# First weights ahead of x, six products ahead of the second tile's transposes, a 22nd weight buffer, and rows numbered by partition in a hybrid attention and expert layer

## The chip, the cores and the metric

The kernel runs on one core of one Trainium2 chip. The metric is the device time of one execution in microseconds (us). The kernel before took 678.57 us (median of 3 runs, 677.72 to 679.63). The engines are TensorE (PE; its weight loads are listed apart as PEld), VectorE (DVE), ScalarE (ACT), GpSimd (POOL) and SyncE (SP), which in this kernel only issues transfers.

## The reference

One layer: two attention branches side by side, merged by gates, and then a mixture of experts. T = 512 tokens, D = 1024, everything in float32.

```python
h = rmsnorm(x, attn_norm)
proj = h @ w_in                                  # one wide product, split into eight parts
c_q, c_kv, k_r, q_b, k_b, v_b, gate_a, gate_b = split(proj)
o_a = mla_attention(c_q, c_kv, k_r, ...)         # 8 heads, low-rank q and kv, causal
o_b = moba_attention(q_b, k_b, v_b, ...)         # 8 heads, causal, block-sparse
x = x + (sigmoid(gate_a) * (o_a @ w_o_mla) + sigmoid(gate_b) * (o_b @ w_o_moba)) @ w_out
x = x + hierarchical_moe(rmsnorm(x, ffn_norm))   # group top-1, then expert top-2 of 8 in the group
return rmsnorm(x, final_norm)

# an expert e, for the tokens routed to it (32 experts in 4 groups, 1024 -> 256 -> 1024)
y = (silu(xb @ w_g[e]) * (xb @ w_u[e])) @ w_d[e]
out[token] += weight * y
```

## The kernel before

Tokens are worked on in four tiles of 128. Float32 products outside the experts are made of three products each: every operand is split into a high part (`hi`) and a low part (`lo`), and hi times hi, hi times lo and lo times hi are added up in PSUM. The high part is cast on ACT, the low part is the rest, made on DVE.

**Start** (`normed_T`, L166 to L185). The tiles of x (x0 to x3, 512 KB each) and three pieces of the first weights (w0 and w1 of two rows of 128 by 352, 352 KB each, and w2 of four, 704 KB) go through SP's queue in the order x0 w0 x1 w1 x2 x3 w2. PE first makes twelve transposes of a constant, then transposes each tile of x (eight blocks of 128 by 128, in two groups of four: "A" and "B"; L206), ACT and DVE split each group (`evac_split`, L44 and L45), and `split` (L65 and L66) splits the weights. The products of the first projection (`proj`, L95 to L97) follow in `mla_compress`. On SP, ACT and DVE the order in this part is as written. PE's order is chosen by the scheduler.

**Middle.** From 14 to 434 us come the projections, both attentions, the gates, the output projection and, tile by tile, the routing (class `Route`), which writes the normed rows to a table in DRAM (`x2d`) and, at the end, the table of routing weights (`Wd`, L591). Small loads for it (`load_late`: the router weights `wr`, the gains `gpj` and `gcol`, the biases and the table of constants `rc`) go through SP early, and the scaling of `wr` on DVE follows them.

**Experts** (`experts`, 434 to 660 us). The 32 experts run as sixteen pairs, q = 0 to 15, with up to 64 tokens for each expert of a pair. A pair needs six weight matrices of 1 MB (gate, up and down for two experts), 96 loads in all, issued by SP into a ring of buffers (`new_w`): the loads of a pair go gate, gate, up, up, down, down, those of pairs 0 to 2 ahead of the loop, those of pair q + 2 at the start of pair q. A load also waits until the third load before it has landed (`load`). The ring has 21 buffers; those numbered 11, 12, 13, 14 and 19 take space of the pool `wp`, which held the split weights until then, and the sixth buffer of that pool is `yhl`, the split output of the experts. For each pair PE transposes the gathered rows (L765), makes the gate and the up products (`gate_up`, L788), transposes the activation (L800) and makes the down products (L815). Pairs in `VIA` send their output through DRAM. The others (0, 3, 6 and 10 to 15) add theirs to x2 with a one-hot matrix S: a combine is two products (L841 and L842) for one half of the columns of one tile, eight combines a pair. The combines of a pair are made during the next pair: `some(n)` makes the next n of those left over.

**End** (`last`). After the last down products the output is split on ACT and DVE (L822, L823), combined, and normed with `final_norm`, whose load goes behind the last weights on SP and which ACT scales first (L973). In this part the order on ACT and DVE is as written.

## Time and profile before

| what | value |
|---|---|
| runs: median, lowest, highest | 678.57, 677.72, 679.63 us |
| the profiled execution | 677.66 us |
| its span in the trace | 675.9 us (1.76 us lie outside it) |
| PE, DVE, ACT, POOL busy | 97%, 53%, 42%, 13% |
| data moved | 155.37 MB, mean 230 GB/s |
| DMA busy share, 7.76 to 434 us and 448 to 652 us | 0.48 and 1.01 |

The profile is taken from one execution; its times are microseconds from the first instruction. A row of a timeline gives the start, the time that the instructions took together (matmuls are pipelined, so that the ends overlap), the engine, the line of the kernel, the operation with its output and inputs, the count, and in brackets the idle time of the engine just before with what ended it. "SPq" and "ACTq" are the queues that issue transfers; the time in such a row is that of issuing. The landing of a transfer is counted from its issue.

### The profile page before, as it was taken

To read this page: it belongs to the slowest core of one execution; us is meant where nothing else is said; L and a number is where in the kernel's file an instruction comes from. 1 tells how busy PE (TensorE), PEld (TensorE's weight loads), DVE (VectorE), ACT (ScalarE), POOL (GpSimd) and SP (SyncE) were. 2 spreads that over 40 slices of the span, in tenths; PEclk is the share of its full clock that TensorE was granted. 3 is DMA by queue.
4 is the path that set the end of the run, shared out by engine and by line. 5 is a ranking of instruction groups with operands and counts; after the bars stand their busy time and mean duration, and the time that the engine had idled before them with its cause. 6 is when DMAs were issued, how large, how long until landed. Compare 5 with 4: busy or idle time off the path is not lost.

```text
span 675.9 us, 11016 instructions
## 1 busy us (share of the span) xinstructions
PE 656.0 (97%) x4150; PEld 502.9 (74%) x4150; DVE 360.5 (53%) x928; ACT 284.9 (42%) x657; POOL 88.2 (13%) x136
## 2 busy tenths in 40 slices
PE   8999999999999999999999999999999999989992
PEld 7998887777788888888888899855566566656551
DVE  4525957877947993434477323733223213556646
ACT  5747545654638683433324143323222222212234
POOL 1504000000000000000000001212112212334303
PEclk9999999999999999999999999999999999999997
DMA  8734451801073028231298957799999999999963
GB/s 264 139 87 73 84 172 63 280 1 63 10 199 104 1 64 249 63 93 63 98 339 300 387 201 262 275 355 417 404 404 419 418 407 409 407 409 408 415 260 128
DMA packets 76041, 155.37 MB, mean 230 GB/s; under 512 B 32270, under 2 KB 54886, under 8 KB 64144
## 3 DMA queue, kind: packets, MB, share of 16 engines
q1 hardware_dynamic: 67424, 141.59, 57.9%
q0 software_dynamic: 5232, 7.98, 3.5%
q10 hardware_dynamic: 3328, 5.05, 2.7%
q8 instruction: 34, 0.56, 0.3%
q14 instruction: 23, 0.19, 0.1%
HBM read 153.24 MB, written 11.60 MB: 244 GB/s over the span
## 4 chain that ended last, share of the span: by engine, by line
PE 86%; DMA 9%; DVE 2%; ACT 1%; POOL 1%; issue 1%; SPq 0%; ACTq 0%
PE yp L815 7%; PE U L788 7%; PE G L788 7%; PE pacc L97 5%; PE pacc L96 5%; PE pacc L95 5%; PE pacc L456 4%; PE pacc L454 4%; PE pacc L455 4%; DMA w<-in_w_exp_gate_dram 4%; DMA w<-in_w_exp_up_dram 4%; PE ptr L425 3%; PE S L407 3%; PE O L433 2%; PE pacc L498 2%; PE pacc L500 2%
## 5 line engine op out<-in xcount | busy, mean ns | idle before, releaser
L66 DVE SCALAR_TENSOR_TENSOR wlo<-wraw,ms,whi 128x256 fp32r<-128x256 f32 (+2 forms) x134 | 68.2, 551 | 30.8 <-ACT whi L65 30.6
L65 ACT ACTIVATE whi<-wraw,ms 128x256 fp32r<-128x256 f32 (+2 forms) x134 | 67.0, 560 | 41.7 <-PE pacc L455 19.8
L95 PE MATMUL pacc<-whi,hThi 128*128 128x352 f32 (+1 forms) x192 | 72.4, 377 | 0.0
L794 DVE SCALAR_TENSOR_TENSOR a<-U,wg,a 128x256 f32<-128x256 f32 x15 | 10.3, 686 | 115.4 <-PE U L788 89.1
L97 PE MATMUL pacc<-whi,hTlo 128*128 128x352 f32 (+1 forms) x192 | 70.1, 365 | 0.0
L96 PE MATMUL pacc<-wlo,hThi 128*128 128x352 f32 (+1 forms) x192 | 70.0, 365 | 0.0
L788 PE MATMUL U<-w,xT 128*64 128x256 f32 x512 | 61.0, 380 | 2.8 <-DMA w<-in_w_exp_up_dram 2.8
L815 PE MATMUL yp<-w,a 128*64 128x512 f32 x256 | 58.5, 598 | 0.5 <-ACT a L802 0.5
L788 PE MATMUL G<-w,xT 128*64 128x256 f32 x512 | 58.0, 379 | 0.0
L788 PEld LDWEIGHTS G<-w,xT 128*64 128x64 f32 x512 | 36.7, 137 | 24.9 <-issue 4.6
L788 PEld LDWEIGHTS U<-w,xT 128*64 128x64 f32 x512 | 37.4, 137 | 23.1 <-DMA w<-in_w_exp_up_dram 4.7
L454 PE MATMUL pacc<-hThi,whi 128*128 128x512 f32 x128 | 50.3, 393 | 0.0
L456 PE MATMUL pacc<-hThi,wlo 128*128 128x512 f32 x128 | 50.3, 393 | 0.0
L455 PE MATMUL pacc<-hTlo,whi 128*128 128x512 f32 x128 | 49.9, 390 | 0.0
L1169 POOL TENSOR_SCALAR sq<-sq 128x1 f32<-128x1 f32 x4 | 0.9, 218 | 343.5 <-ACT junk L1166 343.5
L420 ACT ACTIVATE E<-E,mx 128x128 f32<-128x128 f32 (+3 forms) x64 | 35.6, 557 | 20.4 <-DVE mx L417 19.6
L843 DVE TENSOR_TENSOR x<-x,cp 128x512 f32<-128x512 f32 x64 | 40.0, 682 | 2.0 <-PE cp L842 2.0
L95 PEld LDWEIGHTS pacc<-whi,hThi 128*128 128x128 f32 x192 | 36.1, 188 | 4.9 <-issue 1.4
L815 PEld LDWEIGHTS yp<-w,a 128*64 128x64 f32 x256 | 17.0, 136 | 30.2 <-issue 27.8
L96 PEld LDWEIGHTS pacc<-wlo,hThi 128*128 128x128 f32 x192 | 36.2, 189 | 4.2 <-issue 0.7
L97 PEld LDWEIGHTS pacc<-whi,hTlo 128*128 128x128 f32 x192 | 36.1, 188 | 3.9 <-issue 0.2
L802 ACT COPY a<-G 128x256 f32<-128x256 f32 x16 | 6.0, 373 | 75.2 <-PE G L800 59.0
(245 smaller groups left out, 1354.3 us busy)
## 6 DMA issues: line engine op xcount, KB each, us to landing
w<-in_w_exp_gate_dram SPq DMA_DIRECT2D x32, 1024.0 KB, 8.2
w<-in_w_exp_up_dram SPq DMA_DIRECT2D x32, 1024.0 KB, 8.1
w<-in_w_exp_down_dram SPq DMA_DIRECT2D x30, 1024.0 KB, 8.4
wraw<-in_w_in_dram SPq DMA_DIRECT2D x14, 1024.0 KB, 5.2
wraw<-in_w_out_dram SPq DMA_DIRECT2D x4, 1024.0 KB, 7.3
wraw<-in_w_in_dram SPq DMA_DIRECT2D x5, 704.0 KB, 4.8
xs<-in_x_dram SPq DMA_DIRECT2D x4, 512.0 KB, 6.6
wraw<-in_w_o_mla_dram SPq DMA_DIRECT2D x4, 512.0 KB, 3.5
```

Of the source, the lines that this page charges most:

```text
L65: nc.scalar.mul(hi[:, k], raw[:, k], g)
L66: nc.vector.scalar_tensor_tensor(lo[:, k], raw[:, k], g, hi[:, k].bitcast(F32), ALU.mult, ALU.subtract)
L95: nc.tensor.matmul(ps[t][:, :ncols], act_hi[kk // 4][:, kk % 4, ts], hi[:, k], start=kk == 0, stop=False)
L96: nc.tensor.matmul(ps[t][:, :ncols], act_hi[kk // 4][:, kk % 4, ts], lo[:, k], start=False, stop=False)
L97: nc.tensor.matmul(ps[t][:, :ncols], act_lo[kk // 4][:, kk % 4, ts], hi[:, k], start=False, stop=kk == ktot - 1)
L420: nc.scalar.activation(E, E, AF.Exp, bias=mx, scale=-1.0, accum_out=sm)
L454: nc.tensor.matmul(ps, hi[:, k, ds], self.hT[0][k // 4][:, k % 4], start=k == 0, stop=False)
L455: nc.tensor.matmul(ps, hi[:, k, ds], self.hT[1][k // 4][:, k % 4], start=False, stop=False)
L456: nc.tensor.matmul(ps, lo[:, k, ds], self.hT[0][k // 4][:, k % 4], start=False, stop=k == KD - 1)
L788: nc.tensor.matmul(GU[i][es, 0:256], xT[:, j, es], gu[e][i][:, j * 256:(j + 1) * 256], start=j == 0, stop=j == KD - 1)
L815: nc.tensor.matmul(yp[es], aT[:, j, es], wd[e][:, j * D + half * 512:j * D + half * 512 + 512], start=j == 0, stop=j == 1)
L843: nc.vector.tensor_tensor(self.x2[t][:, hs], self.x2[t][:, hs], cp, ALU.add)
```

## The change

The change has five edits.

- The start sends w0 ahead of x0, so that SP's order is w0 x0 x1 w1 x2 x3 w2. The split of w0 moves ahead of x0's on ACT and DVE. The six products of token tile 0 with w0 (`proj_part`, taken out of `proj`) are written ahead of the second tile's transposes, and a dependence (`earlier`) holds the first of these transposes until the sixth product has ended.
- The pool `wp` ends with the middle part, and its space becomes six buffers of a pool `wx`. Five of them are those of the ring as before. The sixth, `w3`, takes the second up matrix of pair 0, loaded behind the other seventeen loads of pairs 0 to 2, and becomes `yhl` after pair 0's products.
- In pairs whose predecessor left eight combines and is later than the last of `VIA` (pairs 11 to 15), four combines are made between the gate and the up products.
- The rows of the tables `Wd` and `x2d` are numbered by partition (row 4p + t for token p of tile t) instead of by tile (128t + p); the constants `token` and `tm` follow, and `tm` gets 64 more columns.
- Two pads change so that the addresses fit.

```diff
     def proj(self, w, groups, act_hi, act_lo, ncols, evac, gain):
-        ps = [self.acc.tile([P, 512], F32, name="pacc", tag="acc") for _ in range(NT)]
+        first, self.first_ps = self.first_ps, None
+        ps = first or self.new_sums()
...
+                if not (first and k0 == t == 0):
+                    self.proj_part(ps[t][:, :ncols], t, range(k0, k0 + nk), hi, lo, act_hi, act_lo, ktot)
...
+    def proj_part(self, ps, t, ks, hi, lo, act_hi, act_lo, ktot):
+        nc = self.nc
+        ts = slice(t * P, (t + 1) * P)
+        for k, kk in enumerate(ks):
+            nc.tensor.matmul(ps, act_hi[kk // 4][:, kk % 4, ts], hi[:, k], start=kk == 0, stop=False)
+            nc.tensor.matmul(ps, act_hi[kk // 4][:, kk % 4, ts], lo[:, k], start=False, stop=False)
+            mm = nc.tensor.matmul(ps, act_lo[kk // 4][:, kk % 4, ts], hi[:, k], start=False, stop=kk == ktot - 1)
+        return mm
...
-            for t in range(NT):
-                nc.sync.dma_start(xs[t // 2][:, t % 2], io["x"][0, t * P:(t + 1) * P, :])
-                if t != 2:
+            for t in ("w", 0, 1, "w", 2, 3, "w"):
+                if t == "w":
                     k, n = groups[len(raw)]
                     raw.append(self.load_raw(self.w_in_view(CC // 3 * 2, CC // 3)(k, n), (n, CC // 3)))
+                else:
+                    nc.sync.dma_start(xs[t // 2][:, t % 2], io["x"][0, t * P:(t + 1) * P, :])
...
+            self.first_w.append(self.split(raw[0], g[:, 0, 0:2]))
+            mm = None
             for t in range(NT):
                 x = xs[t // 2][:, t % 2]
-                self.transpose_split(x[:, 0:512], 4, self.hT, 0, t)
-                if t < 2:
-                    self.first_w.append(self.split(raw[t], g[:, 0, 2 * t:2 * t + 2]))
+                self.transpose_split(x[:, 0:512], 4, self.hT, 0, t, mm)
+                if t == 0:
+                    self.first_ps = self.new_sums()
+                    mm = self.proj_part(self.first_ps[0][:, 0:CC // 3], 0, range(2), *self.first_w[0], *self.hT, KD)
+                if t == 1:
+                    self.first_w.append(self.split(raw[1], g[:, 0, 2:4]))
                 self.started = self.transpose_split(x[:, 512:D], 4, self.hT, 4, t)
...
-            nc.scalar.dma_start(self.Wd.rearrange("(t p) c -> p t c", p=P), self.W)
+            nc.scalar.dma_start(self.Wd.rearrange("(p t) c -> p t c", p=P), self.W)
...
-        pool, tag = {11: (self.wp, "wraw"), 12: (self.wp, "wraw"), 13: (self.wp, "whi"), 14: (self.wp, "wlo"),
-                     19: (self.wp, "wlo")}.get(i, (self.big, "big"))
-        return pool.tile([P, 2048], F32, name="w", tag=tag)
+        at = {11: 0, 12: 1, 13: 2, 14: 4, 19: 5}.get(i)
+        if at is not None:
+            return self.wx.tile([P, 2048], F32, name="w", tag=f"w{at}")
+        return self.big.tile([P, 2048], F32, name="w", tag="big")
...
-            ws = [[self.load_rows(io[n][0, e]) for e in range(2)] for n in ("w_exp_gate", "w_exp_up")]
-            return list(zip(*ws))
+            g = [self.load_rows(io["w_exp_gate"][0, e]) for e in range(2)]
+            return [(g[0], self.load_rows(io["w_exp_up"][0, 0])), (g[1], self.wx.tile([P, 2048], F32, name="w", tag="w3"))]
...
-        self.yhl = self.wp.tile([P, 2048], F32R, name="yhl", tag="whi")
+        self.load_rows(self.io["w_exp_up"][0, 1], wgu[0][1][1])
...
+                    if j == KD - 1 and len(todo) == 8 and q - 1 not in VIA and q > VIA[-1]:
+                        some(4)
...
+                if q == 0:
+                    self.yhl = self.wx.tile([P, 2048], F32R, name="yhl", tag="w3")
...
-        nc.scalar.dma_start(L.x2d[self.ts, c0:c1], self.x2[:, c0:c1])
+        nc.scalar.dma_start(L.x2d.rearrange("(p t) c -> p t c", p=P)[:, self.t, c0:c1], self.x2[:, c0:c1])
...
-    rc[:, 33:33 + NT] = np.arange(P)[:, None] + P * np.arange(NT)[None, :] - 1024
+    rc[:, 33:33 + NT] = NT * np.arange(P)[:, None] + np.arange(NT)[None, :] - 1024
```

Line numbers of the changed kernel differ: L206 becomes L221, L95 to L97 become L106 to L108, L788 becomes L806, L841 and L842 become L859 and L860, L697 becomes L715.

PE's order at the start, before (`ptr<-ident` are transposes of the constant, `ptr<-ident,xs` those of x, `pacc` the products of the first projection):

```order
1 L160 MATMUL ptr<-ident 128x128 x12
2 L206 MATMUL ptr<-ident,xs 128x128 x12
3 L95 MATMUL pacc<-whi,hThi 128x352
4 L206 MATMUL ptr<-ident,xs 128x128 x4
5 L96 MATMUL pacc<-wlo,hThi 128x352
6 L97 MATMUL pacc<-whi,hTlo 128x352
7 L95 MATMUL pacc<-whi,hThi 128x352
8 L96 MATMUL pacc<-wlo,hThi 128x352
9 L97 MATMUL pacc<-whi,hTlo 128x352
10 L95 MATMUL pacc<-whi,hThi 128x352
11 L96 MATMUL pacc<-wlo,hThi 128x352
12 L206 MATMUL ptr<-ident,xs 128x128 x4
```

And in the changed kernel:

```order
1 L169 MATMUL ptr<-ident 128x128 x12
2 L221 MATMUL ptr<-ident,xs 128x128 x8
3 L106 MATMUL pacc<-whi,hThi 128x352
4 L107 MATMUL pacc<-wlo,hThi 128x352
5 L108 MATMUL pacc<-whi,hTlo 128x352
6 L106 MATMUL pacc<-whi,hThi 128x352
7 L107 MATMUL pacc<-wlo,hThi 128x352
8 L108 MATMUL pacc<-whi,hTlo 128x352
9 L221 MATMUL ptr<-ident,xs 128x128 x12
10 L106 MATMUL pacc<-whi,hThi 128x352
11 L107 MATMUL pacc<-wlo,hThi 128x352
12 L106 MATMUL pacc<-whi,hThi 128x352
```

Before, x0's and half of x1's transposes stood ahead of the first product. Now the six products stand between x0's eight transposes and the twelve of x1 and x2's first half.

SP's queue of expert loads around the last loads of pairs 0 to 2, before (`w_4369` is the second up matrix of pair 0; `w_4397` is the last down matrix of pair 2, and `w_4508` the first gate matrix of pair 3):

```order
86 L697 DMA w_4367<-in_w_exp_up_dram 128x8x256 [waits PE_49]
87 L697 DMA w_4369<-in_w_exp_up_dram 128x8x256 [waits Pool_49]
...
106 L697 DMA w_4395<-in_w_exp_down_dram 128x2048 [waits DMAHW6_49,PE_49]
107 L697 DMA w_4397<-in_w_exp_down_dram 128x2048 [waits DMAHW0_49,DMAHW4_49,PE_49,Pool_49]
108 L697 DMA w_4508<-in_w_exp_gate_dram 128x2048 [waits DMAHW2_49,PE_49,Pool_49]
109 L697 DMA w_4510<-in_w_exp_gate_dram 128x2048 [waits DMAHW6_49,PE_49]
110 L697 DMA w_4512<-in_w_exp_up_dram 128x2048 [waits DMAHW5_49,DMAHW0_49]
```

And in the changed kernel (`w_4379` is that second up matrix, `w_4518` the first gate matrix of pair 3):

```order
85 L715 DMA w_4377<-in_w_exp_up_dram 128x8x256 [waits PE_49]
86 L715 DMA w_4380<-in_w_exp_down_dram 128x2048 [waits Pool_49]
...
105 L715 DMA w_4406<-in_w_exp_down_dram 128x2048 [waits DMAHW6_49,DMAHW2_49,PE_49]
106 L715 DMA w_4379<-in_w_exp_up_dram 128x8x256 [waits DMAHW7_49,DMAHW3_49,PE_49]
107 L715 DMA w_4518<-in_w_exp_gate_dram 128x2048 [waits DMAHW0_49,Pool_49]
108 L715 DMA w_4520<-in_w_exp_gate_dram 128x2048 [waits DMAHW5_49,DMAHW2_49,Pool_49]
109 L715 DMA w_4522<-in_w_exp_up_dram 128x2048 [waits DMAHW3_49]
```

The matrix moves from second of the up loads to the eighteenth place, and the loads between move one forward.

PE's order in the last pair, before (G and U are the gate and up products, `cp` and `sum` the combines of pair 14):

```order
2075 L788 MATMUL G<-w,xT 64x256 x16
2076 L788 MATMUL U<-w,xT 64x256 x16
2077 L841 MATMUL cp<-yhl,S 128x512
2078 L842 MATMUL cp<-yhl,S 128x512
2079 L841 MATMUL cp<-yhl,S 128x512
2080 L842 MATMUL cp<-yhl,S 128x512
2081 L837 MATMUL sum<-yhl,S 128x512 x4
2082 L841 MATMUL cp<-yhl,S 128x512
2083 L842 MATMUL cp<-yhl,S 128x512
2084 L800 MATMUL G<-ident,a 128x128 x2
```

And in the changed kernel:

```order
2075 L806 MATMUL G<-w,xT 64x256 x16
2076 L859 MATMUL cp<-yhl,S 128x512
2077 L860 MATMUL cp<-yhl,S 128x512
2078 L859 MATMUL cp<-yhl,S 128x512
2079 L860 MATMUL cp<-yhl,S 128x512
2080 L855 MATMUL sum<-yhl,S 128x512 x4
2081 L806 MATMUL U<-w,xT 64x256 x16
2082 L859 MATMUL cp<-yhl,S 128x512
2083 L860 MATMUL cp<-yhl,S 128x512
2084 L859 MATMUL cp<-yhl,S 128x512
```

Eight products, four combines, stand ahead of the up products instead of behind them; the same holds in pairs 11 to 14.

## Rows read from the trace of the kernel before

**Rows 1.** The page, first part: busy us, share of the span, instructions of each engine.
```profile
PE 656.0 (97%) x4150; PEld 502.9 (74%) x4150; DVE 360.5 (53%) x928; ACT 284.9 (42%) x657; POOL 88.2 (13%) x136
```

**Rows 2.** Windows: length, busy of PE, PEld, DVE, ACT, POOL, PEclk, DMA, GB/s.
```profile
7.76:434.00 426.24, 424.90 (x2544) 362.89 (x2546) 260.07 (x754) 215.63 (x507) 25.13 (x61) 1.00 0.48 151
434.00:448.00 14.00, 13.54 (x104) 7.82 (x106) 5.78 (x24) 4.50 (x9) 4.19 (x4) 1.00 0.70 220
448.00:652.00 204.00, 201.15 (x1436) 121.12 (x1432) 78.93 (x128) 52.10 (x118) 51.49 (x49) 1.00 1.01 407
4.40:5.90 1.50, 1.50 (x8) 1.50 (x8) 0.00 (x0) 0.36 (x1) 0.00 (x0) 1.00 0.99 349
```

**Rows 3.** Waits of SP and PE in the expert stage: us in total, times, longest.
```profile
SPq L697 <- DMA w<-in_w_exp_up_dram: 56.8, 23, 3.9
...
PE U L788 <- DMA w<-in_w_exp_up_dram: 2.8, 3, 1.8
```

**Rows 4.** Timeline of PE at the start.
```profile
4.39 1.94 PE L206 MATMUL ptr<-ident,xs 128*128 128x128 f32 x8
7.76 0.63 PE L206 MATMUL ptr<-ident,xs 128*128 128x128 f32 x4 [1.43 <-DMA xs<-in_x_dram]
8.14 0.41 PE L95 MATMUL pacc<-whi,hThi 128*128 128x352 f32 x1
...
9.14 0.32 PE L95 MATMUL pacc<-whi,hThi 128*128 128x352 f32 x1
9.30 0.32 PE L96 MATMUL pacc<-wlo,hThi 128*128 128x352 f32 x1
```

**Rows 5.** Timeline of SP's queue at the start.
```profile
0.74 0.39 SPq L166 DMA_DIRECT2D xs<-in_x_dram  x1
1.20 0.42 SPq L49 DMA_DIRECT2D wraw<-in_w_in_dram  x1
1.66 0.47 SPq L166 DMA_DIRECT2D xs<-in_x_dram  x1
```

**Rows 6.** Landings of these three (x0, x1, w0): count, KB, us from the issue.
```profile
xs<-in_x_dram SPq DMA_DIRECT2D x1, 512.0 KB, 3.6
...
xs<-in_x_dram SPq DMA_DIRECT2D x1, 512.0 KB, 6.0
wraw<-in_w_in_dram SPq DMA_DIRECT2D x1, 352.0 KB, 5.1
```

**Rows 7.** Timeline of ACT at the start.
```profile
5.54 0.59 ACT L44 CAST hThi<-ptr 128x512 fp32r<-128x512 f32 x1 [2.81 <-PE ptr L206]
```

**Rows 8.** Timeline of DVE at the start, and at its rope products.
```profile
6.16 0.69 DVE L45 TENSOR_TENSOR hTlo<-ptr,hThi 128x512 fp32r<-128x512 f32 x1 [6.16 <-ACT hThi L44]
...
21.89 0.53 DVE L113 SCALAR_TENSOR_TENSOR rope<-pacc,ms,ropet 128x32 f32<-128x32 f32 x3 [3.95 <-ACT craw L244]
```

**Rows 9.** Timeline of SP's queue where the loads of pair 4 begin.
```profile
448.00 0.80 SPq L697 DMA_DIRECT2D w<-in_w_exp_gate_dram  x2
```

**Rows 10.** Timeline of PE at the end of pair 0.
```profile
442.44 1.16 PE L765 MATMUL ptr<-ident,xg 128*128 128x128 f32 x8
...
444.32 3.65 PE L815 MATMUL yp<-w,a 128*64 128x512 f32 x16 [0.46 <-ACT a L802]
```

**Rows 11.** Timeline of POOL, the gather of pair 1's rows.
```profile
434.63 1.18 POOL L746 DMA_INDIRECT xg<-x2d,xi  x1 [5.21 <-DMA w<-in_w_exp_up_dram]
```

**Rows 12.** Landing of this gather, us from the issue.
```profile
xg<-x2d,xi POOLq DMA_INDIRECT x1, 3.7
```

**Rows 13.** The chain of waits in pair 14, one product of a combine.
```profile
636.28 0.23 PE cp L842
```

**Rows 14.** Timeline of SP's queue, its last load.
```profile
650.30 0.60 SPq L1022 DMA_DIRECT2D fin<-in_final_norm_dram  x1
```

**Rows 15.** Landing of this load: KB, us from the issue.
```profile
fin<-in_final_norm_dram SPq DMA_DIRECT2D x1, 512.0 KB, 6.9
```

**Rows 16.** Timeline of ACT behind the last down products.
```profile
657.29 1.06 ACT L973 ACTIVATE fin<-fin 128x1024 f32<-128x1024 f32 x1 [1.61 <-issue]
658.25 0.67 ACT L822 ACTIVATE yhl<-yp,sw 128x512 fp32r<-128x512 f32 x1
```

More of the change, by code (lines that the diff above doesn't have):

```diff
@@ L91, in proj, with new_sums @@
             for t in range(NT):
-                ts = slice(t * P, (t + 1) * P)
-                for k in range(nk):
-                    kk = k0 + k
-                    nc.tensor.matmul(ps[t][:, :ncols], act_hi[kk // 4][:, kk % 4, ts], hi[:, k], start=kk == 0, stop=False)
-                    nc.tensor.matmul(ps[t][:, :ncols], act_hi[kk // 4][:, kk % 4, ts], lo[:, k], start=False, stop=False)
-                    nc.tensor.matmul(ps[t][:, :ncols], act_lo[kk // 4][:, kk % 4, ts], hi[:, k], start=False, stop=kk == ktot - 1)
-                if kk == ktot - 1:
+                if not (first and k0 == t == 0):
+                    self.proj_part(ps[t][:, :ncols], t, range(k0, k0 + nk), hi, lo, act_hi, act_lo, ktot)
+                if k0 + nk == ktot:
                     evac(t, ps[t])
             k0 += nk
+    def new_sums(self):
+        return [self.acc.tile([P, 512], F32, name="pacc", tag="acc") for _ in range(NT)]
+    def proj_part(self, ps, t, ks, hi, lo, act_hi, act_lo, ktot):
[6 more added lines that the diff above has]
+        return mm
     def rope(self, dst, src, cc, ss, nh, half, f, tmp=None):
@@ L132, in setup @@
         self.eps = c.tile([P, 1], F32, name="eps")
-        c.tile([P, 16], F32, name="pad")
+        c.tile([P, 48], F32, name="pad")
         nc.gpsimd.memset(self.eps, EPS * D)
@@ L196, in norm_power, with transpose_split @@
         nc.gpsimd.tensor_tensor(r, r, self.mhalf, ALU.pow)
-    def transpose_split(self, src, nblk, dst, k0, t):
+    def transpose_split(self, src, nblk, dst, k0, t, earlier=None):
         nc = self.nc
@@ L205, in transpose_split @@
             for j in range(n):
-                nc.tensor.transpose(ps[:, j * P:(j + 1) * P], src[:, (g + j) * P:(g + j + 1) * P], self.ident)
+                tr = nc.tensor.transpose(ps[:, j * P:(j + 1) * P], src[:, (g + j) * P:(g + j + 1) * P], self.ident)
+                if earlier is not None and g == j == 0:
+                    self.after(tr, earlier)
             i, o = divmod(k0 + g, 4)
@@ L672, in route_setup @@
         self.after(nc.gpsimd.dma_start(self.tri, io["tri"]), self.started)
-        self.tm = c.tile([P, T], F16, name="tm")
+        self.tm = c.tile([P, T + 64], F16, name="tm")
         self.after(nc.gpsimd.dma_start(self.tm, io["tm"]), self.started)
@@ L705, in load_w, with load_rows @@
         return w
[L707 to L709 removed]
+    def load_rows(self, src, w=None):
+        w = self.new_w() if w is None else w
         self.load(w.rearrange("p (j f) -> p j f", j=KD), src.rearrange("(j p) f -> p j f", p=P))
@@ L1095, in overflow_pair @@
         hit = self.mp.tile([P, 512], F32, name="ptr", tag="m")
-        nc.vector.scalar_tensor_tensor(hit, zb, slot, self.tm, ALU.is_equal, ALU.mult, accum_out=xf)
+        nc.vector.scalar_tensor_tensor(hit, zb, slot, self.tm[:, 0:T], ALU.is_equal, ALU.mult, accum_out=xf)
         xi = self.row_index()
@@ L1138, in run @@
             self.attn_out()
+        self.wx = ctx.enter_context(tc.tile_pool(name="wx", bufs=1, side="right", **SB))
+        for i in range(6):
+            self.wx.tile([P, 2048], F32, name="w", tag=f"w{i}")
         self.gp = ctx.enter_context(tc.tile_pool(name="gp", bufs=1, **PS))
```

11 lines of the change are left out of this document (5 added, 6 removed).

## The prediction, made before the changed kernel was run

> **What bounds the kernel now.** I read the page's busy shares first: TensorE (PE) is busy for 97% of the span, the next engine for 53% [rows 1]. Shares over the whole span mix stages, so next come the windows. From 434 to 448 us, where the first expert pair runs, the DMA engines are busy 0.70 of the time at 220 GB/s: that stretch has room. From 448 to 652 us the share is 1.01 at 407 GB/s and PE is busy 201.15 of 204 us: both are full, and one has to see which of them waits [rows 2]. The waits say it. SP, which issues the weight loads, waits for nothing but its own earlier loads (56.8 us on up weights alone, and nearly as much on each of the other two kinds), and PE waits 2.8 us in three places, each time for up weights [rows 3]. So the stage from 448 us to the last load is set by the DMA engines, with PE a few tenths to two microseconds ahead. Last I read the first 14 us: PE does eight transposes of x's first tile from 4.39 to 6.33 us, waits 1.43 us for the second tile, and from 7.76 us it has no gap [rows 4]. Everything between 7.76 us and about 434 us is PE work end to end, 424.90 us busy of 426.24 [rows 2], so what the start loses is lost for good, and nothing but the 1.43 us can be won there.
>
> **Part 1, the start.** The change lets w0 (352 KB, the first weights) leave before x's tiles, puts the six products of token tile 0 with w0 ahead of the second tile's transposes, and holds those transposes until the sixth product has ended.
> Before, x0 was issued at 0.74 and landed 3.6 us later (4.34), w0 at 1.20 and 5.1 later (6.30), x1 at 1.66 and 6.0 later (7.66) [rows 5, 6]. The same 1376 KB now travel as w0, x0, x1. So x1 still lands at about 7.66, but x0 has the bytes of w0 and of itself ahead of its end, as w0 had before: it lands at about 6.3 instead of 4.34.
> From there the chain is serial. Transposes from 6.35. The second group of four (x1) took 0.63 us, and the next product followed after 0.38 us; x0's own eight took 1.94, which is twice as long for each [rows 4]. The high half is cast on ACT 1.15 us after the first transpose (5.54 − 4.39) [rows 7], the low half starts on DVE 0.62 later and takes 0.69 [rows 8]. The third of the six products needs that low half, and from there four products remain, 0.16 us apart (9.14 and 9.30) and 0.32 long [rows 4]. At the quicker rate the four transposes end 0.63 after their start: cast at 7.0, low half 7.6 to 8.3, last product issued by 8.8 and ended, with its own 0.32 us and the release, at about 9.2. That is when x1's transposes start, against 7.76. Of the 1.44 us difference 0.96 is work done ahead (six products), so 0.5 is lost. A second gap follows: the transposes of x2's second half need a PSUM buffer that x1's low half frees. x1's first four end at 9.8, cast and low half end at 11.1, and PE has only eight transposes and three products, 1.2 us, to put there: 0.4 to 0.6 more. Loss 1.1 us. If transposes and products both go at the rate that x0's transposes show, the cast is at 7.5, the low half ends at 8.8, four products take 1.2 and x1 starts at 10.4: 1.7 + 0.4 = 2.1 us.
> The range of this term: 2.3 lost (2.1 and a first packet 0.2 late), and 0.6 won if x0 landed early enough (by about 4.8) that x1's own landing were the limit, since 0.96 would be done ahead and the 0.4 gap stays. I take 1.4 lost: the order of the bytes speaks against an early x0, and the two rates are about equally likely, with the quicker one somewhat ahead because the granted clock of that stretch reads 1.00, the upper of the two levels, 2.4 GHz [rows 2].
> The Trainium skill ("TensorE: Matmul & The Clock Gate", Part 1: The HAM clock gate) says that an engine which has been idle falls back to half rate and that the time of the transition varies from run to run. By the clock column no slow stretch exists here, by the doubled transposes one does; by the rule the change, which lengthens PE's idle time ahead of 6.35, would lose the 2.1, by the column 1.1. The trace does not settle it.
> On DVE the routing rows (scaled router weights) now stand ahead of the rope products and of the next weights' low halves, and wait for small loads that used to be needed later. DVE has 3.95 us of idle time just ahead of the rope products at 21.89 [rows 8], which covers them; cost 0, at worst 0.5, taken 0.
>
> **Part 2, the 22nd buffer.** The buffer that later holds the split output (yhl) now first takes the second up matrix of pair 0, which is loaded last of the first eighteen loads. So the loads behind the old place all move one forward. Before, pair 4's gate loads left at 448.00, right behind the end of pair 0's down products (444.32 + 3.65 = 447.97) [rows 9, 10]. After yhl has taken its buffer the ring is as large as before, and pair 4's loads still wait for the same products. So the extra buffer fills only idle time before 448 us and cannot pull the full stretch behind it forward by a load. What it can give is an emptier queue at 448: part of the load then in flight, for which I take 0.3 us, with 0 and 1.0 as ends (a load of 1 MB is 2.6 us at 407 GB/s). Its price is that 424 to 441 us now carries one more load back to back, and the gather of pair 1's rows, issued at 434.63 [rows 11] and landed in 3.7 us [rows 12], shares it. PE wants these rows at 442.44 [rows 10], so the gather has 7.8 us. With two loads of 2.6 ahead of its 3.7 it would need 8.9: 0 to 1.1 us of stall, and I take 0.2, near the row's own 3.7. Pair 0's second up matrix arrives well before its products.
>
> **Part 3, combines between gate and up products.** In pairs 11 to 15 four of the eight combines (two products each, 0.23 us a product [rows 13]) move ahead of the up products. They fill the time in which PE would wait for up weights, so the 2.8 us of PE waits go, but PE's waits were not the bound there: the loads land when they land, and the last ones set the end. What would count is the last pair: 8 products, 1.85 us, are done before its up products instead of behind them. But the last down products are followed by the split on ACT, and ACT has the scaling of final_norm ahead of it in its order: that load leaves at 650.30 and lands 6.9 us later, at 657.2 [rows 14, 15]; the scaling starts at 657.29, takes 1.06, and the split starts at 658.25 [rows 16]. The load is the last on a full queue and nothing moves it. So the tail gains 0, at best the full 1.85.
>
> **Part 4, layout.** Rows numbered by partition make the write of the routing weights 128 rows of 528 B instead of 512 of 132 B; it waits for nothing new and 4 us of slack stand behind it. The longer table of slot numbers, the pads and the new addresses move the same bytes. Cost 0.
>
> **Sum**, on the profiled execution: span 675.9, and 1.76 outside it, 677.66. Start +1.4, DVE 0, gather +0.2, emptier queue −0.3, tail 0, layout 0: +1.3, so 679.0. The median of the runs shown, 678.57, lies 0.91 above this execution, so the forecast is 679.9; the rivals' times are put on the median in the same way.
>
> **The rivals.**
> A, the combines pay in full. For it: they are the only PE work removed from behind the last loads. Against it: the split that the last combines wait for starts as soon as the scaling of final_norm lets it, whatever PE does. It would give 1.4 + 0.2 − 0.3 − 1.85 = −0.55, so 678.0.
> B, slower: x0's late landing at the slow rate. Its place is the first 11 us, the price 2.1 us, and it decides, with 0.2 us or more from the gather, as soon as the transposes of x0 take 1.9 us again; with the crowded gather (up to 1.1) behind it, 2.1 + 1.1 − 0.3 = +2.9, 681.5; with the gather at its 0.2 it is +2.0, 680.6. For it: the only transposes of x0 that the trace shows were slow. Against it: the clock column.
> C, the 22nd buffer pulls the full stretch forward by one load. That is 2.6 us: 1.4 + 0.2 − 2.6 = −1.0, so 677.6. For it: the stretch is bound by DMA and the one ahead is at 0.70. Against it: the loads at 448.00 wait for pair 0's buffers.
> D, the change does at the start what its order suggests: w0 overlaps with x0 and the 1.43 us gap is filled. 0.6 to 1.0 won instead of 1.4 lost: −0.8 + 0.2 − 0.3 = −0.9, 677.7; with A's tail 675.8. Against it: the bytes ahead of x0's end.
>
> **How the numbers follow.** Forecast 0.50, A 0.12, B 0.15, C 0.08, D 0.15. A measurement of this kernel tells about 0.3%, 2.0 us, from no change: faster means below 676.5, slower above 680.6. Faster needs D with A or C, nearly all of D's chance: 0.13. Slower is four fifths of B and the upper end of the forecast (a sum over +2.0): 0.12 + 0.13 = 0.25. Same: 0.62. The range: below, D and C without their best cases, 677.0; above, B with its gather, 682.0.
>
> **What would show it.** In the changed profile: x0's first transpose near 6.35 us; x1's near 9.2 (10.4 for B, 7.8 for D); an idle of some 0.4 us ahead of the transposes of x2's second half; pair 4's gate loads behind pair 0's down products as before, so about 1 us later; no waits of PE for up weights in pairs 12 to 15; final_norm's scaling on ACT directly ahead of the last split. The forecast is wrong if x0 lands before 5.5, if the DMA share at 434 to 448 reaches 0.9 and the first load behind it leaves earlier than 448.0, or if the last combine starts more than 1 us earlier relative to the last load's landing.

## The result, and the profile of the changed kernel

The changed kernel takes 681.61 us (median of 8 runs, 680.03 to 685.14), the kernel before 678.08 (8 runs beside it, 677.03 to 679.63): a ratio of 1.0057, with a 95% interval of 1.0043 to 1.0070. It is slower, by 3.5 us. The forecast was 679.9 and the range held, but the likeliest case had it 1.3 us slower, which is no change to a measurement of this kernel; what came is nearest to rival B.

The profiled execution took 680.29 us, span 678.5, so it shows 2.6 us of the loss. PE on the page, against [rows 1]:

```profile
PE 659.2 (97%) x4150; PEld 504.4 (74%) x4150; DVE 361.6 (53%) x928; ACT 284.9 (42%) x657; POOL 87.3 (13%) x136
```

The start, PE's timeline, against [rows 4]:

```profile
6.01 1.97 PE L221 MATMUL ptr<-ident,xs 128*128 128x128 f32 x8 [1.49 <-DMA xs<-in_x_dram]
...
8.98 0.49 PE L106 MATMUL pacc<-whi,hThi 128*128 128x352 f32 x1
9.28 0.49 PE L107 MATMUL pacc<-wlo,hThi 128*128 128x352 f32 x1
9.57 0.49 PE L108 MATMUL pacc<-whi,hTlo 128*128 128x352 f32 x1
9.87 2.73 PE L221 MATMUL ptr<-ident,xs 128*128 128x128 f32 x12
...
15.26 0.60 PE L221 MATMUL ptr<-ident,xs 128*128 128x128 f32 x4
```

x0 is there at 6.0 instead of 4.4. Its eight transposes take as long as before, but this time the products behind them are slow too, 0.30 us apart instead of 0.16, and so are the next twelve transposes. The last of x's transposes, which started at 12.88 before, start at 15.26: 2.4 us later. Before:

```profile
12.88 0.60 PE L206 MATMUL ptr<-ident,xs 128*128 128x128 f32 x4
```

DVE, against the second of [rows 8]:

```profile
24.95 0.17 DVE L673 TENSOR_SCALAR gpj<-gpj 128x8 f32<-128x8 f32 x1 [4.64 <-DMA gpj<-in_ffn_norm_dram]
...
27.03 0.18 DVE L698 CAST iotaU<-rc 128x32 uint32<-128x32 f32 x1 [1.02 <-DMA rc<-in_rconst_dram]
27.12 0.53 DVE L122 SCALAR_TENSOR_TENSOR rope<-pacc,ms,ropet 128x32 f32<-128x32 f32 x3
```

The rope products, at 21.89 before, wait for routing constants that nobody needs yet. Behind them stand the low halves of the next weights; PE, 2.36 late at 14 us, is 2.67 late from 40 us on, another 0.3 us net. Pair 0's gate products start 2.64 late, at 436.53 instead of 433.89:

```profile
433.89 3.67 PE L788 MATMUL G<-w,xT 128*64 128x256 f32 x32
```

Pair 0 and pair 1, PE and then POOL, against [rows 10, 11]:

```profile
436.53 3.67 PE L806 MATMUL G<-w,xT 128*64 128x256 f32 x32
...
446.31 1.16 PE L783 MATMUL ptr<-ident,xg 128*128 128x128 f32 x8 [1.16 <-DMA xg<-x2d,xi]
447.30 0.38 PE L818 MATMUL G<-ident,a 128*128 128x128 f32 x2
448.15 3.65 PE L833 MATMUL yp<-w,a 128*64 128x512 f32 x16 [0.46 <-ACT a L820]
```

```profile
436.79 1.18 POOL L764 DMA_INDIRECT xg<-x2d,xi  x1 [4.72 <-DVE yw L888]
```

Its landing, against [rows 12], and what SP's queue does in that stretch, against [rows 9]:

```profile
xg<-x2d,xi POOLq DMA_INDIRECT x1, 9.5
```

```profile
427.70 8.23 SPq L715 DMA_DIRECT2D w<-in_w_exp_gate_dram  x2
435.98 0.91 SPq L715 DMA_DIRECT2D w<-in_w_exp_up_dram  x2
440.65 6.91 SPq L715 DMA_DIRECT2D w<-in_w_exp_down_dram  x2
451.83 0.80 SPq L715 DMA_DIRECT2D w<-in_w_exp_gate_dram  x2
```

The gather lands 9.5 us after its issue instead of 3.7, because three loads of 1 MB leave in the 1.2 us ahead of it. PE waits 1.16 us and is 3.83 us late from there (444.32 to 448.15). Why the loads come in a bunch stands in SP's waits from 415 to 452 us:

```profile
SPq L715 <- DMA x2d<-x: 21.3, 4, 7.3
SPq L715 <- DMA Wd<-W: 6.2, 1, 6.2
```

Before, SP waited there for PE (its longest wait, 8.5 us, was for the product at L620) and for its own loads. Now it waits for two kinds of writes with whose data the loads have nothing to do (buffer_pool_writes below tests this). The trace says how: SP's loads and ACT's writes signal the same eight completion semaphores, and each of these loads leaves when the last transfer that had its own semaphore has landed. The second gate load of pair 3 has that of the last write of normed rows (issued 427.80, landed 435.5, the load left at 435.60); the last down load of pair 3 has that of the write of the routing weights. Before, these loads had semaphores whose last transfers were long done.

The end, SP and ACT, against [rows 14, 16], and PE's last down products, first of the changed kernel, then of the kernel before:

```profile
653.25 0.60 SPq L1044 DMA_DIRECT2D fin<-in_final_norm_dram  x1
```

```profile
660.18 1.06 ACT L995 ACTIVATE fin<-fin 128x1024 f32<-128x1024 f32 x1 [2.29 <-DMA fin<-in_final_norm_dram]
661.14 1.25 ACT L840 ACTIVATE yhl<-yp,sw 128x512 fp32r<-128x512 f32 x2
```

```profile
657.91 3.65 PE L833 MATMUL yp<-w,a 128*64 128x512 f32 x16
```

```profile
656.17 3.65 PE L815 MATMUL yp<-w,a 128*64 128x512 f32 x16
```

The combines do fill PE's waits (0.3 us for up weights are left of 2.8, [rows 3]), and PE is only 1.74 us late at its last down products. But ACT waits 2.29 us for final_norm, the split starts 2.89 late, and 1.15 of the 2.09 us that the combines had won are gone. The loads themselves are 3.83 late at 451.83 and 2.95 at 653.25: 0.9 came back. In sum 2.64 (start and DVE) + 1.19 (gather) − 2.09 (combines) + 1.15 (final_norm) = 2.89 at the split, 2.6 at the end.

### The profile page after: what moved, and what is told of

Read it like the earlier page. It is cut to its first block, busy times and chain, and to the rows that moved or that the text cites. A ratio compares the mean times of both kernels' runs of the same rounds, so it can differ in the third digit from the quotient of the medians.

```text
span 678.5 us, 11014 instructions
## 1 busy us (share of the span) xinstructions
PE 659.2 (97%) x4150; PEld 504.4 (74%) x4150; DVE 361.6 (53%) x928; ACT 284.9 (42%) x657; POOL 87.3 (13%) x136
## 4 chain that ended last, share of the span: by engine, by line
PE 83%; DMA 9%; DVE 3%; ACT 2%; issue 1%; POOL 1%; SPq 0%; ACTq 0%; POOLq 0%
PE yp L833 7%; PE U L806 6%; PE G L806 6%; PE pacc L107 5%; PE pacc L108 5%; PE pacc L106 5%; PE pacc L471 4%; PE pacc L473 4%; PE pacc L472 4%; DMA w<-in_w_exp_down_dram 4%; PE ptr L442 3%; PE S L424 3%; PE O L450 2%; DMA w<-in_w_exp_gate_dram 2%; PE pacc L515 2%; PE pacc L517 2%
## 5 line engine op out<-in xcount | busy, mean ns | idle before, releaser
L106 PE MATMUL pacc<-whi,hThi 128*128 128x352 f32 (+1 forms) x192 | 72.9, 380 | 0.0
L108 PE MATMUL pacc<-whi,hTlo 128*128 128x352 f32 (+1 forms) x192 | 70.4, 367 | 0.0
L806 PE MATMUL U<-w,xT 128*64 128x256 f32 x512 | 59.2, 380 | 0.3 <-DMA w<-in_w_exp_up_dram 0.3
L806 PE MATMUL G<-w,xT 128*64 128x256 f32 x512 | 59.3, 380 | 0.0
L806 PEld LDWEIGHTS G<-w,xT 128*64 128x64 f32 x512 | 37.2, 137 | 25.6 <-issue 4.9
L806 PEld LDWEIGHTS U<-w,xT 128*64 128x64 f32 x512 | 37.4, 137 | 19.1 <-issue 1.8
L106 PEld LDWEIGHTS pacc<-whi,hThi 128*128 128x128 f32 x192 | 36.4, 190 | 5.1 <-issue 1.4
L108 PEld LDWEIGHTS pacc<-whi,hTlo 128*128 128x128 f32 x192 | 36.3, 189 | 4.1 <-issue 0.2
```

What stands on the lines that cost most here:

```text
L106: nc.tensor.matmul(ps, act_hi[kk // 4][:, kk % 4, ts], hi[:, k], start=kk == 0, stop=False)
L108: mm = nc.tensor.matmul(ps, act_lo[kk // 4][:, kk % 4, ts], hi[:, k], start=False, stop=kk == ktot - 1)
L806: nc.tensor.matmul(GU[i][es, 0:256], xT[:, j, es], gu[e][i][:, j * 256:(j + 1) * 256], start=j == 0, stop=j == KD - 1)
```

## The experiments

My theory after this: the start costs 2.4 to 2.7 us, the 22nd buffer 1.2, and the combines gain nothing because of final_norm. The rivals: the loss sits in the expert stage alone, or the layout brings it. Ratios are to the kernel before on the same chip, with 95% intervals.

**start_undone**: the changed kernel with the old start.

```diff
-            for t in ("w", 0, 1, "w", 2, 3, "w"):
+            for t in range(NT):
...
-                if t == 0:
-                    self.first_ps = self.new_sums()
-                    mm = self.proj_part(self.first_ps[0][:, 0:CC // 3], 0, range(2), *self.first_w[0], *self.hT, KD)
```

> The changed kernel with the start as before (x0 first on SP, w0's split behind x0's, no six products ahead, no held transposes); the 22nd buffer, the combines and the layout stay. My theory: the shift of PE against before is 0 up to about 440 us (in the changed kernel it is +2.36 at 14 us and +2.67 from 40 us on), the gather of pair 1 still makes PE wait about 1.2 us ahead of its transposes, and the end is 0 to 0.4 us later than before, because the last load (final_norm) sets it: ratio to before 1.000 (0.999 to 1.001). Rival 1, the loss of the changed kernel sits in the expert stage: ratio 1.003 or more. Rival 2, the combines pay in full once the start is undone: 2 us less at the end, ratio 0.997.

1.0020 (0.9996 to 1.0044), between my theory and rival 1; the interval holds both no change and 1.003. The start's share of the shift is gone (PE 0.1 us early up to 440 us), but the gather's wait is 1.97, and behind it comes something that I had not foreseen. PE, and windows of 2 us (columns as in [rows 2]):

```profile
444.35 1.16 PE L778 MATMUL ptr<-ident,xg 128*128 128x128 f32 x8 [1.97 <-DMA xg<-x2d,xi]
...
446.19 5.35 PE L828 MATMUL yp<-w,a 128*64 128x512 f32 x16 [0.46 <-ACT a L815]
```

```profile
444.00:446.00 2.00, 1.38 (x10) 1.14 (x10) 0.46 (x1) 0.84 (x3) 0.44 (x1) 1.00 0.74 258
446.00:448.00 2.00, 1.81 (x6) 0.68 (x8) 0.56 (x2) 0.13 (x1) 1.57 (x2) 0.62 0.82 311
448.00:450.00 2.00, 2.00 (x6) 0.48 (x4) 0.00 (x0) 0.35 (x1) 1.00 (x1) 0.52 0.79 304
450.00:452.00 2.00, 2.00 (x14) 0.86 (x12) 0.75 (x1) 0.73 (x2) 0.00 (x0) 1.00 0.02 3
```

The granted clock, 1.00 (2.4 GHz) up to 446 us, falls to its lower level (1.2 GHz) behind the idle time, and the down products take 5.35 us instead of 3.65. So the wait costs PE twice here: 2.0 and 1.7. Not every such wait does: the clock fell behind waits of 1.97 us here and 1.26 us in long_warm, and stayed at 1.00 behind 1.54 us in no_hold and 1.16 us in the changed kernel's profiled execution. Whether it fell in other executions of the changed kernel, whose median lies 1.3 above its profile, is not shown.

**long_warm**: the changed kernel, PE kept busy until x0 lands.

```diff
-        for i in range(12):
+        for i in range(18):
             nc.tensor.transpose(warm[:, 0:P], self.ident, self.ident)
```

> The changed kernel with 18 instead of 12 transposes of the constant at the very start, so that PE is busy from 1.7 us to about 5.9 us, when x0 lands. Theory 1 (PE's rate in the first 12 us depends on what PE did before, and the idle 1.5 us ahead of x0 made it slow): x0's eight transposes take about 0.9 instead of 1.8 us, the products follow each other by 0.16 instead of 0.30, x1's transposes start near 8.6 instead of 9.87, and the kernel is about 1.2 us faster than the changed one (ratio to before near 1.004 where the changed one has 1.0057). Theory 2 (slow because x0 has just landed or because transfers are still running): the transposes take 1.8 us as before, and nothing is gained.

Theory 1 holds for the start:

```profile
5.97 1.38 PE L221 MATMUL ptr<-ident,xs 128*128 128x128 f32 x8 [0.17 <-DMA xs<-in_x_dram]
...
8.74 0.32 PE L107 MATMUL pacc<-wlo,hThi 128*128 128x352 f32 x1
8.90 0.32 PE L108 MATMUL pacc<-whi,hTlo 128*128 128x352 f32 x1
9.05 1.47 PE L221 MATMUL ptr<-ident,xs 128*128 128x128 f32 x12
```

The products are 0.16 apart and the twelve transposes take 1.47 instead of 2.73; at 14 us PE is 0.56 late instead of 2.36. So x0's late landing costs some 0.6 us at the quick rate, and the slow rate 1.8 more. Of what is won DVE's wait takes a part: from 40 to 430 us PE is 1.25 late instead of 2.67. The ratio is 1.0039 (1.0021 to 1.0057), as expected, but its interval reaches up to the changed kernel's 1.0057, so the trace shows the gain and the time does not. This profile's down products of pair 0 take 5.35 us again.

**no_hold**: the changed kernel without the dependence.

```diff
-                self.transpose_split(x[:, 0:512], 4, self.hT, 0, t, mm)
+                self.transpose_split(x[:, 0:512], 4, self.hT, 0, t)
```

> The changed kernel without the dependence that holds x1's transposes until the sixth product has ended (PE's order is then two of x1's transposes ahead of the first product, and two of them behind the second). It tells how much of the start's loss is the hold and how much x0's late landing. If the late landing is the cause, PE is still 2 us or more late at 40 us (2.67 in the changed kernel); if the hold is, the shift at 40 us falls below 1 us.

One run, 679.12 us. PE is 1.05 late between 60 and 400 us: neither bound that I had written (under 1, over 2) was met. x0's transposes start at 6.02 as in the changed kernel, and PE is 1.6 less late. How much of that is the hold stays open: the rate rises near 9.4 in this profile and near 12.5 in that of the changed kernel, and where it rises differs between profiles of one and the same start (gather_first below). DVE's order differs too: its wait for `rc` stands behind two groups of rope products here.

**start_only**: the kernel before with the new start alone, as in the change (the longer `tm` and the pad beside the constants stay in).

```diff
-            for t in range(NT):
+            for t in ("w", 0, 1, "w", 2, 3, "w"):
```

> The kernel before with the new start alone (w0 first on SP, six products ahead, x1's transposes held). Theory: PE is 1.2 us late at 40 us where its rate rises early and 2.7 us where it rises late, nothing later in the kernel gives any of it back or adds to it, so the median is 1.2 to 2.7 us above that of the kernel before: ratio 1.0018 to 1.004. Rival (the start's loss disappears later, in the stage set by the DMA engines): ratio 1.000 to 1.001.

1.0051 (1.0033 to 1.0069), above the range of my theory: the start's loss alone is as large as that of the whole change. In its profile PE is 1.89 late at 12 to 25 us and 3.47 from 30 us on. The step is the wait of DVE for `rc`, longer than in the changed kernel, and PE's idle time with it:

```profile
27.75 0.18 DVE L698 CAST iotaU<-rc 128x32 uint32<-128x32 f32 x1 [1.71 <-DMA rc<-in_rconst_dram]
27.85 0.53 DVE L122 SCALAR_TENSOR_TENSOR rope<-pacc,ms,ropet 128x32 f32<-128x32 f32 x3
```

```profile
28.52 0.40 PE L106 MATMUL pacc<-whi,hThi 128*128 128x352 f32 x1 [0.47 <-DVE rope L122]
```

This profile also says what the slow products of the start are. x0's eight transposes take 1.10 us here, the quick rate; from the fourth product on the products are 0.30 apart, as in the changed kernel, and here the granted clock reads it, the lower level (1.2 GHz):

```profile
9.23 0.50 PE L108 MATMUL pacc<-whi,hTlo 128*128 128x352 f32 x1
```

```profile
8.50:11.80 3.30, 3.30 (x15) 3.23 (x15) 0.90 (x2) 1.18 (x3) 0.00 (x0) 0.50 1.02 401
```

**buffer_only**: the kernel before with the 22nd buffer alone, as in the change.

```diff
-        self.yhl = self.wp.tile([P, 2048], F32R, name="yhl", tag="whi")
+        self.load_rows(self.io["w_exp_up"][0, 1], wgu[0][1][1])
```

> The kernel before with the 22nd buffer alone (second up matrix of pair 0 loaded eighteenth, into the space of yhl). My theory: three loads of 1 MB are in flight when pair 1's rows are gathered, the gather lands after about 9.5 us instead of 3.7, PE waits 1.2 us there, pair 4's loads leave 1.2 us later, and 0.9 of it comes back because less is in flight at 448 us: the end is 0.3 us later, ratio 1.0004 (1.000 to 1.002). Rival 1: the gather's delay in the changed kernel comes from the new row numbers, so here the gather lands after 4 us, no wait, and the end is 0.9 us earlier (ratio 0.9987). Rival 2: the loads behind it gain a whole load, 2.5 us (ratio 0.996).

1.0047 (1.0027 to 1.0067), far off all three. The profile shows the wait for the gather (0.88 us), but PE is then only 0.6 late until 580 us; the rest comes behind that, as 4.2 us of PE's waits for up weights, because the loads are late: 0.57 at 448 us, 1.4 at 453, and 2.3 at the end. SP's waits name the beginning of it: the last down load of pair 3 left at 446.18 instead of 442.96, after 8.5 us of waiting for the routing weights' write:

```profile
SPq L698 <- DMA x2d<-x: 16.5, 4, 7.2
SPq L698 <- DMA Wd<-W: 8.5, 1, 8.5
```

The same two microseconds, here and in the kernel before:

```profile
444.00:446.00 2.00, 1.54 (x10) 0.67 (x11) 1.02 (x2) 0.83 (x3) 0.00 (x0) 1.00 0.16 52
```

```profile
444.00:446.00 2.00, 1.68 (x8) 0.63 (x10) 0.65 (x2) 0.26 (x1) 1.70 (x2) 1.00 0.90 365
```

So the DMA engines, which the buffer was to keep busy, stand at 0.16 at 444 us where they had 0.90 before. In the changed kernel they read 1.04 there and 0.87 or more up to 452 us: PE is 3.8 us late by then, and the same waits leave no hole. What is added between 453 us and the end is not traced to anything; layout_only, without the buffer, has as much of PE's waits.

**gather_first**: start_undone, and the up loads of pair 3 behind the gather.

```diff
+        if len(self.loads) == 20:
+            self.after(d, self.gathers[0])
```

> The changed kernel with the start as before, and with the up loads of pair 3 held until the gather of pair 1's rows has landed. Theory 1 (the gather is slow because three loads of 1 MB are ahead of it, and PE's wait for it costs twice, once as a wait and once because the granted clock falls behind it): the gather lands 4 to 6 us after its issue at 434.0, PE has no wait ahead of pair 1's transposes, pair 0's down products take 3.65 us in every execution, and against the kernel with the start undone (ratio 1.002) the time falls by 2 to 3.5 us: ratio to before 0.997 to 1.000. Theory 2 (the new row numbers or the write of the routing weights make the gather slow): it still lands after 9 us and PE waits 2 us, ratio 1.002.

The gather lands in 3.5 us, PE's wait for it is gone and the down products take 3.65 us, as theory 1 has it; the ratio, 1.0023 (1.0007 to 1.0039), is not better, so the time of theory 1 did not come. In this profile the old start itself ran at the slow rate, and PE was 2.8 us late by 14 us; the end is 2.1 late, 0.7 ahead of what that start alone leaves. Whether most executions of this kernel start so I can't tell from one profile: open.

```profile
7.74 1.08 PE L216 MATMUL ptr<-ident,xs 128*128 128x128 f32 x4 [1.30 <-DMA xs<-in_x_dram]
...
10.35 0.49 PE L106 MATMUL pacc<-whi,hThi 128*128 128x352 f32 x1
```

**fill_wait**: start_undone with work for PE in the gather's wait.

```diff
+                    for i in range(16):
+                        nc.tensor.transpose(idle[:, 0:P], self.ident, self.ident)
                     next_rows()
```

> The changed kernel with the start as before, and with 16 transposes of the constant (1.8 us of PE work whose output nobody reads) ahead of pair 1's transposes, where PE waits for the gather. Theory (the wait is followed by a stretch at the lower clock because PE was idle): the gather lands as late as with the start undone, but PE's idle time ahead of the transposes falls from 2.0 to about 0.2 us, the granted clock stays at 1.00 from 446 to 450 us, the down products take 3.65 instead of 5.35 us, and the spread of the times falls: all of them near 678, ratio 0.999 to 1.000 where the start undone has 1.002. Rival (the slow down products come from the transfers of that stretch): they take 5.35 us as before, ratio 1.002.

PE's down products take 3.65 us and the windows from 446 to 452 us read 1.00, as the theory has it; one profile is weak evidence here, since the clock also stayed up behind two of the waits named above. The ratio, 1.0028 (1.0013 to 1.0042), misses: PE is 1.4 late from 448 us on (some 0.6 of it because the gather has landed at 443.4 and the filling ends at 444.0), gains 2 with the combines, and final_norm's load, 1.9 late, sets the end. Neither this run nor gather_first is better than start_undone: what PE wins at the gather does not reach the end while the last load comes late.

**combine_only**: the kernel before with the combines alone.

```diff
+                    if j == KD - 1 and len(todo) == 8 and q - 1 not in VIA and q > VIA[-1]:
+                        some(4)
```

> The kernel before with the four combines between gate and up products alone. My theory: PE's waits for up weights (2.8 us) go, PE is some 2 us earlier from 600 us on, and ahead of the last split all of it is given back in the wait for final_norm's scaling on ACT: the end is 0 to 0.2 us earlier, ratio 1.000. Rival: the end is 1.85 us earlier, ratio 0.997.

0.9994 (0.9974 to 1.0014), as expected: PE is about 2 us early from 600 us on, and the median is not. The profiled execution ends 1.0 us earlier than that of the kernel before, with final_norm's load leaving 0.55 earlier; the rival's 0.997 lies outside the interval.

**combine_late_scaling**: combine_only, with final_norm's scaling behind the first split.

```diff
-            nc.scalar.mul(self.fin[:, 0], self.fin[:, 0], D ** 0.5)
             yp = [self.down_products(dn, aT, h, (self.mp, "m")) for h in range(2)]
             y = [self.down_split(yp[0], sw, 0)]
+            nc.scalar.mul(self.fin[:, 0], self.fin[:, 0], D ** 0.5)
```

> The kernel before with the four combines between gate and up products, and with final_norm's scaling on ACT moved behind the split of the first half of the last output. My theory (that scaling, waiting for the last load, is what holds the tail): the last split starts 1.7 us earlier and the end comes 1.5 us earlier than in the kernel before, ratio 0.9978 (0.9965 to 0.999); the combines alone gave 0.9994. Rival (the last down weights hold PE just as long): the end moves by less than 0.3 us, ratio 0.9995.

0.9983 (0.9968 to 0.9999). The interval holds the rival's 0.9995 too, and overlaps with that of combine_only; the trace decides. The split starts at 656.30 instead of 658.25 and the scaling no longer stands ahead of it:

```profile
656.30 0.69 ACT L822 ACTIVATE yhl<-yp,sw 128x512 fp32r<-128x512 f32 x1 [2.06 <-PE yp L815]
656.88 1.05 ACT L977 ACTIVATE fin<-fin 128x1024 f32<-128x1024 f32 x1
```

**layout_only**: the kernel before with the new row numbers alone, as in the change.

```diff
-            nc.scalar.dma_start(self.Wd.rearrange("(t p) c -> p t c", p=P), self.W)
+            nc.scalar.dma_start(self.Wd.rearrange("(p t) c -> p t c", p=P), self.W)
```

> The kernel before with the new row numbers alone (128 rows of 528 B in the write of the routing weights, constants and table lengths). Theory: nothing on the path changes, ratio 1.000 (0.999 to 1.001); the write of the routing weights lands within 4.5 us as before. Rival (the start undone has ratio 1.002 though it holds the 22nd buffer, which alone had 1.0047, so the layout gives 1 us or more): ratio 0.998.

1.0010 (0.9999 to 1.0022): nothing gained. The write of the routing weights lands in 2.3 us instead of 4.5, beside the path; the profile's end is 1.4 late with PE waits of 4.3 us for up weights that I can't lay at the layout's door. Its last load leaves 1.4 late and that of combine_late_scaling 0.8 early, both without the 22nd buffer: the full stretch ends that differently from profile to profile, and one profile's end tells no more than that.

**fill_start**: combine_late_scaling with six transposes of the constant in PE's gap at 6.3 us.

```diff
+                if t == 1:
+                    for i in range(6):
+                        nc.tensor.transpose(warm[:, 0:P], self.ident, self.ident)
```

> The kernel before with the combines between gate and up products and the late scaling of final_norm (ratio 0.9983), and with six transposes of the constant between x0's and x1's transposes, so that PE has no idle time from 1.7 us on. Theory (where PE's rate rises depends on what PE did before; with idle time ahead of x1 it sometimes rises only near 13 us, at a cost of up to 2.8 us): the rate is high from x1's transposes on in every execution, the slowest runs come down by 1 to 2 us, the median by 0.5 to 1: ratio 0.997. Rival (the rate has nothing to do with the idle time): ratio 0.9983 as without them, or 0.9985, if the six delay x1 by 0.1 us.

0.9972 (0.9959 to 0.9986), 676.77 us: better than the kernel before and the changed one. Whether the six transposes have a part in it is not shown: the interval holds the rival's 0.9983, and the profile's start is as quick as the old start is in seven of eight profiles. All runs compared but one (678.5) lie between 675.6 and 676.9; without the six transposes, on another chip, they spread from 675.7 to 679.1, but buffer_pool_writes, which has the six too, spreads from 676.0 to 678.5.

**buffer_pool_writes**: fill_start with the 22nd buffer, and with the writes on POOL's queue.

```diff
-            nc.scalar.dma_start(self.Wd.rearrange("(t p) c -> p t c", p=P), self.W)
+            nc.gpsimd.dma_start(self.Wd.rearrange("(t p) c -> p t c", p=P), self.W)
```

> The kernel of fill_start (old start with six filling transposes, combines between gate and up products, late scaling; ratio 0.9972) with the 22nd buffer added, and with the writes of the normed rows and of the routing weights issued by POOL instead of ACT. In the changed kernel SP's loads of pairs 2 and 3 wait 21.3 us for the writes of the normed rows and 6.2 us for that of the routing weights, with which they share a completion semaphore but no data. Theory (these waits bunch three loads ahead of pair 1's gather and hold the last load of pair 3): on POOL's queue the writes have semaphores of their own, SP has no such wait, the gate loads of pair 3 leave ahead of 432 us, pair 1's gather lands within 7 us and PE waits less than 0.5 us for it; ratio 0.996 to 0.9975, no worse than without the buffer. Rival (one load more ahead of the gather is enough, whatever SP waits for): PE waits 0.9 us or more, ratio 0.9985 to 1.002.

SP has no wait for the writes, both gate loads of pair 3 leave by 426.4, while the write of normed rows issued at 425.68 lands 7.6 us later (so the loads need nothing of it), and PE does not wait for the gather, although it still needs 8.0 us, one more than expected:

```profile
425.42 1.01 SPq L701 DMA_DIRECT2D w<-in_w_exp_gate_dram  x2
```

```profile
442.81 1.16 PE L769 MATMUL ptr<-ident,xg 128*128 128x128 f32 x8
```

0.9978 (0.9963 to 0.9993). Free of these waits the buffer costs nothing that can be told against fill_start's 0.9972, and gives nothing: the stage behind it is full, as the prediction had it. final_norm's load leaves at 650.39, where it left at 650.30 before and 1.9 to 3.9 us later in all kernels that have the buffer and the shared semaphores.

## Why the prediction was right, and where it was not

- **x0 lands late, and PE cannot give it back.** Right: x0's first transposes at 6.01 (6.35 forecast), x1's at 9.87 (9.2 or 10.4). The size was wrong, since I took 1.4, between the rates; it was the slow one, 2.4 (forecast 2.1; the quick one, forecast 1.1, was 0.6 in long_warm). It was also made up otherwise: x1's transposes started 2.11 later, of which 0.96 is work done ahead, so 1.15 was lost there instead of 1.7; the second gap, 0.4, did not come; and the twelve transposes behind took 2.73 us where long_warm's took 1.47, a price of 1.26 that no term held. The clock column decided against it and was no witness: it read 1.00 through a stretch with products 0.30 apart, and start_only, with the same spacing, reads 0.50. The Trainium skill ("TensorE: Matmul & The Clock Gate", Part 1: The HAM clock gate) has the half rate as the default; activity releases it, and idle time brings it back. That agrees with long_warm, quick with 0.17 us of idle time ahead of x0 instead of 1.49; but idle time alone does not decide, since the kernel before is quick right behind 1.43 us of it [rows 4].
- **The DVE term, "cost 0, at worst 0.5, taken 0".** This failed. I took the 3.95 us of idle time ahead of the rope products for cover; but what DVE now waits for lands 5 us behind them. It cost PE 0.3 net in the changed kernel, still within the 0.5, but 0.8 in long_warm and 1.6 in start_only.
- **The gather.** Forecast 0 to 1.1, taken 0.2; 1.16 measured. Right in its cause (loads ahead of it), wrong in their number: three, not two. The price can have a second part that no term held, the lower clock behind the wait (1.7 us in start_undone and long_warm, nothing in the changed kernel's profile).
- **What held the loads.** I had read the waits for data and buffers, not those for a completion semaphore that a write of another queue had used last. That a load moved one place changes which transfers it waits for was no part of the working.
- **The queue behind 448 us, −0.3 with −1.0 as an end.** 0.9 came back in the changed kernel, but in buffer_only the loads went from 0.57 late to 2.3, and without the buffer the stretch ends between 0.8 earlier (combine_late_scaling) and 1.4 later (layout_only); so no run shows the term. Rival C did not come.
- **The tail, 0.** Right for loads that come on time: in combine_only PE's 2 us do not reach the median, and in combine_late_scaling the split takes them. In the changed kernel 1.15 of 2.09 were given back; the rest counted, because PE (3.83 late) was further behind than final_norm's load (2.95).
- **The sum** was 1.3, measured 3.5 between the medians, 2.6 between the profiles. The range held because its upper end was rival B's, and B's two prices are what came: 2.4 for its 2.1 at the start, 1.2 for its 1.1 at the gather. That the total lies so near B's is partly luck, since the start's price came in other parts, DVE's wait, the semaphores and the combines are not in it, and no run explains the 0.9 by which the medians differ more than the profiles. The parts alone (+0.51%, +0.47%, −0.06%, +0.10%) add up to more than the whole. The traces suggest why, without showing it: the end is the later of PE's work and the loads, and a loss of the one partly hides in the other, as the hole in the loads at 444 us in buffer_only is not there in the changed kernel.

## What to carry to other kernels

A transfer that is moved ahead on a full queue delays what it overtakes by its own bytes; ask whether PE can begin with it alone. An idle stretch of TensorE can have two prices, its length and the rate behind it; a few transposes that nobody reads can fill it, but the runs here that did so (long_warm, fill_wait, fill_start) show a gain in the trace at most, and none in the time beyond noise. When loads are reordered, list for each what its queue waits for, the shared completion semaphores too; and before work is moved into a wait, look for the next thing that ends last, here a load and its place in ACT's order.

## What the runs showed of the hardware

- PE's rate near the start differs between executions of the same start: with the old one the transposes of x1 took 0.63 us for four in one profile [rows 4] and 1.08 in gather_first, while the granted clock read 1.00 in both. In start_only, with the same slow spacing of products (0.30 us), it read 0.50. So at the start of a trace the spacing of equal instructions is the better witness.
- After 2.0 us without work, and 0.46 more a microsecond later, the granted clock read 0.62 and 0.52 in the next two windows of 2 us, and 1.00 in the one behind them (start_undone). After 1.54 us and 0.46 us it stayed at 1.00 (no_hold).
- A gather of 128 rows landed in 3.7 us with one load of 1 MB in flight (the kernel before) and in 9.5 us with three that had just left (the changed kernel).
- SP's loads and ACT's writes shared eight completion semaphores: in the changed kernel the loads waited up to 7.3 us at a time for writes with which they share no data. With the writes on POOL's queue they did not.
